# Eight transposes in two visits instead of four in four: the hand-over of finished activations in an encoder's feed-forward on one core

## The chip, the cores and the metric

One core of a Trainium2 chip. The metric is the device time of one execution in microseconds (us), as the median of runs. TensorE does the matmuls and the transposes, ScalarE (ACT in the rows) and VectorE (DVE) empty the accumulators and prepare weights, GpSimd (POOL) and SyncE (SP) issue transfers. PEld is TensorE's weight load, which runs beside its matmuls.

## What is computed

Two layers of an encoder on 512 tokens of width 1024; the first mixes the tokens by dilated window attention, the second by gated linear attention. Each mixer is followed by the same feed-forward, which the change touches:

```python
def swiglu(h, w_gate_up, w_down):
    g, u = jnp.split(h @ w_gate_up, 2, axis=-1)
    return (jax.nn.silu(g) * u) @ w_down
# every layer: h = h + mixer(rms_norm(h)); h = h + swiglu(rms_norm(h))
# FFN_HIDDEN = 2816, everything float32
```

## The kernel before

**Numbers in two halves.** A float32 operand is split into a rounded part (`wh`, `xh`; made by ScalarE, L96) and the rest (`wl`, `xl`; made by VectorE, L97), and a product is three matmuls: high by high, low by high, high by low. In `product` these are L329, L330 and L331.

**The first half of the feed-forward** is `gate_up`. The 2816 hidden columns of gate and of up are done in six chunks, j = 0 to 4 with 512 columns and j = 5 with 256. In each chunk the blocks of `h @ w_gate_up` come from seven block products instead of eight (Strassen's scheme, with sums of blocks of h, `S1` to `S4`, made beforehand, and sums of blocks of the weights, made while they load). The seven products stand in this order: A11, A12, S1, S2, S4, S3, A22. Each is 24 matmuls of 128x512 (128x256 in the last chunk) on two weight tiles of 128x1024. They share three pairs of PSUM banks: A11, S2, S3 and A22 go to `b1`, A12 to `b2` (both with the tag `pp`, printed as ppp), S1 and S4 to `b3` (tag `s`, printed as ps). Between products ScalarE copies a bank out (`copy`, L368), and VectorE combines the copies (L382, L410, L411, L420, L432). S3 and A22 are both summed into `b1`, and `b1` is copied between them: A22 may write a bank only when L368 has read it.

**The hand-over.** At the end of a chunk `done = (h1, h2)` holds its activations, tokens on the partitions. The second half of the feed-forward needs them turned. `turn(c)` does a quarter of a chunk: four transposes of 128x128 (L354, matmuls against an identity) into one PSUM bank, two of `h1` and two of `h2`, and one copy by ScalarE (L356). The bank is `pt` for even c and `po` for odd c, one buffer each. The quarters of chunk j-1 are turned during chunk j: `turn(0)` after A11, `turn(1)` after A12, `turn(2)` after S1, `turn(3)` after S2. The very last chunk's two quarters are turned at the end of `gate_up`, which the change leaves alone. Per layer that is 22 quarters, 88 transposes, on both layers 176.

**What sets the order.** Each engine works through its own instructions in a fixed order, which a scheduler sets when the program is built: among the instructions that it holds to be ready it takes the one with the highest priority, and priority falls in the order of the code. `with self.tc.issue_after(x)` makes it place the instructions inside after x. Only `turn(0)` stands in such a block (after `self.multiplied`, the last matmul of A11).

**Weights.** `forms` loads and sums the weight tiles of a chunk. Three buffers each of `wh` and `wl` go round: the split of a tile (L96, then L97) can start when the tile three places earlier has been multiplied. The tiles of S4 and S3 share their raw buffers `wB`: once S4's two tiles are split, an adding transfer issued by GpSimd (L252, for each tile when its L97 has ended) turns them into S3's, which are then split again. Chunks 1 to 4 work this way.

Of the kernel before, what the change touches and what calls it, by code (L numbers as in the profile page):

```python
# [39 lines left out]
class Trunk:  # L40
# [292 lines left out]
    def gate_up(self, layer, acts):  # L333
# [15 lines left out]
        def turn(c):  # L349
            if done is None:  # L350
                return
            pt = self.p("to"[c % 2])
            for i in range(NT):
                nc.tensor.transpose(pt[:, i * P:(i + 1) * P], done[i // 2][:, i % 2, c * P:(c + 1) * P], self.ident)  # L354
            a = self.t("h") if len(acts) < KT else late[len(acts) - KT]
            ACT(a, pt, AF.Copy)  # L356
            acts.append(a)

        for j in range(6):
# [5 lines left out]
            def copy(src):  # L365
                out = keep()
                for i in range(2):
                    self.copied = ACT(out[:, i, 0:width], src[i][:, 0:width], AF.Copy)  # L368
                return out
# [2 lines left out]
            self.product(b1, A11, first if j == 0 else next(w), width, True)  # L372
            with self.tc.issue_after(self.multiplied.ins):
                turn(0)
            g1 = copy(b1)
            b2 = pair("pp")
            self.product(b2, A12, next(w), width, True)
            turn(1)
            def gates():
                for i in range(2):  # L380
                    e = g1[:, i, 0:width]
                    DVE.tensor_add(e, b2[i][:, 0:width], e)  # L382
                    ACT(e, e, AF.Silu, scale=R[:, i:i + 1])
# [6 lines left out]
                with self.tc.issue_after(self.low.ins):  # L390
                    self.last_sums()
            self.product(b3, S1, x5, width, True)
            turn(2)
            p5 = copy(b3)
            x6 = next(w)
            if j == 0:
# [1 line left out]
                    for m in range(KT):  # L398
                        self.add_square(m, self.h[m], ("sq", "R")[m % 2])
            self.product(b1, S2, x6, width, False)  # L400
            turn(3)
            if j == 0:
                R = self.token_norm()
                with self.tc.issue_after(self.on_dve.ins):
# [821 lines left out]
```

## Time and profile before

| what | value |
|---|---|
| median of 3 runs | 1508.99 us (1508.53 to 1509.37) |
| the profiled execution, its own time | 1508.64 us |
| its span, first to last instruction | 1506.8 us |
| TensorE busy | 1491.7 us, 99% of the span |
| VectorE, ScalarE, GpSimd busy | 63%, 52%, 7% |
| granted TensorE clock, mean | 1.000 |

The span is the part of the execution in which instructions run; the 1.8 us between it and the time lie around it. A row of a timeline gives the start, the duration, the engine, the line and the operation with what it writes and reads, and in brackets the idle time of the engine before it and what ended that. Matmuls overlap: a 128x512 matmul is printed with 0.39 us and the next one starts 0.23 us later, so costs on TensorE are read from starts, not from durations.

### The profile page before, as it was taken

What the parts mean: (1) busy time and instruction counts of PE and PEld (TensorE: products, weight loads), DVE (VectorE), ACT (ScalarE), POOL (GpSimd) and SP (SyncE); (2) the same over time, 40 slices, a digit from 0 to 9 for tenths busy, and PEclk for the clock granted to TensorE, in tenths of its full rate; (3) what the DMA queues carried; (4) which work ended last, traced back from release to release, by engine and by line L of the source; (5) the groups of instructions that cost most, each with busy time, mean ns of one, the idle gap of its engine ahead of it and who ended that gap; (6) DMA issues with size and microseconds to landing.
All of it is one profiled execution on the core that took longest, in us unless ns stands there. A gap on an engine that the chain in (4) does not pass through costs nothing.

```text
span 1506.8 us, 21145 instructions
## 1 busy us (share of the span) xinstructions
PE 1491.7 (99%) x8142; PEld 1225.9 (81%) x8142; DVE 947.9 (63%) x1728; ACT 781.8 (52%) x1348; POOL 110.3 (7%) x192
## 2 busy tenths in 40 slices
PE   8999999999999999999999999999999999999998
PEld 6878787887877878888888887888888888888887
DVE  6584766777476778866667334837476866668222
ACT  6353453545466655755567233545644855568121
POOL 0001010101010010211110000000010211110000
PEclk9999999999999999999999999999999999999999
DMA  8423222243222136777674333212156676675331
GB/s 281 158 67 94 81 79 84 85 128 99 74 71 71 44 121 194 224 168 156 148 162 129 92 100 96 91 56 78 46 157 188 195 170 153 156 152 147 118 110 60
DMA packets 59829, 183.95 MB, mean 122 GB/s; under 512 B 10032, under 2 KB 10608, under 8 KB 59728
## 3 DMA queue, kind: packets, MB, share of 16 engines
q1 hardware_dynamic: 44912, 133.17, 27.0%
q0 software_dynamic: 14816, 49.42, 16.4%
q8 instruction: 64, 1.05, 0.3%
q14 instruction: 37, 0.30, 0.1%
HBM read 174.11 MB, written 8.46 MB: 121 GB/s over the span
## 4 chain that ended last, share of the span: by engine, by line
PE 87%; DVE 8%; ACT 2%; DMA 1%; issue 1%; SPq 0%; ACTq 0%; DVEq 0%
PE ppp L109 9%; PE ppp L108 9%; PE ppp L110 9%; PE ppp L549 8%; PE ppp L550 8%; PE ppp L548 8%; PE ppp L329 6%; PE ppp L330 6%; PE ppp L331 6%; PE ps L331 2%; PE ps L329 2%; PE ps L330 2%; PE po L680 2%; PE ps L640 1%; DVE wl L97 1%
## 5 line engine op out<-in xcount | busy, mean ns | idle before, releaser
L97 DVE TENSOR_TENSOR wl<-wf,wh 128x1024 fp32r<-128x1024 f32 (+1 forms) x184 | 220.6, 1200 | 229.8 <-ACT wh L96 229.0
L96 ACT ACTIVATE wh<-wf 128x1024 fp32r<-128x1024 f32 (+1 forms) x184 | 191.3, 1040 | 326.7 <-PE ppp L109 195.2
L548 PE MATMUL ppp<-wh,xs 128*128 128x512 f32 (+1 forms) x672 | 256.7, 386 | 5.5 <-ACT wh L96 5.5
L549 PE MATMUL ppp<-wl,xs 128*128 128x512 f32 (+1 forms) x672 | 257.7, 383 | 0.7 <-DVE wl L97 0.3
L550 PE MATMUL ppp<-wh,xs 128*128 128x512 f32 (+1 forms) x672 | 257.5, 383 | 0.0
L548 PEld LDWEIGHTS ppp<-wh,xs 128*128 128x128 f32 x672 | 126.6, 189 | 32.4 <-ACT wh L96 5.5
L549 PEld LDWEIGHTS ppp<-wl,xs 128*128 128x128 f32 x672 | 126.8, 189 | 26.5 <-DVE wl L97 2.9
L550 PEld LDWEIGHTS ppp<-wh,xs 128*128 128x128 f32 x672 | 126.8, 189 | 25.0 <-issue 1.3
L97 DVE TENSOR_TENSOR wl<-wA,wh 128x1024 fp32r<-128x1024 f32 x88 | 107.6, 1222 | 37.8 <-ACT wh L96 37.8
L96 ACT ACTIVATE wh<-wA 128x1024 fp32r<-128x1024 f32 x88 | 93.2, 1059 | 62.1 <-PE ppp L331 45.8
L329 PE MATMUL ppp<-wh,a 128*128 128x512 f32 (+1 forms) x288 | 108.1, 381 | 0.0
L108 PE MATMUL ppp<-xs,wh 128*128 128x512 f32 x272 | 107.4, 396 | 0.0
L330 PE MATMUL ppp<-wl,a 128*128 128x512 f32 (+1 forms) x288 | 107.4, 373 | 0.0
L331 PE MATMUL ppp<-wh,a 128*128 128x512 f32 (+1 forms) x288 | 107.3, 374 | 0.0
L109 PE MATMUL ppp<-xs,wh 128*128 128x512 f32 x272 | 106.6, 393 | 0.0
L110 PE MATMUL ppp<-xs,wl 128*128 128x512 f32 x272 | 106.0, 391 | 0.0
L97 DVE TENSOR_TENSOR wl<-wB,wh 128x1024 fp32r<-128x1024 f32 x38 | 46.5, 1225 | 73.7 <-ACT wh L96 73.7
L628 ACT ACTIVATE sm<-sm,st 128x160 f32<-128x160 f32 (+2 forms) x128 | 56.8, 447 | 40.9 <-DVE st L627 40.8
L329 PE MATMUL ps<-wh,sh 128*128 128x512 f32 (+1 forms) x192 | 73.1, 381 | 0.0
L329 PE MATMUL ppp<-wh,sh 128*128 128x512 f32 (+1 forms) x192 | 72.2, 376 | 0.0
L331 PE MATMUL ppp<-wh,sl 128*128 128x512 f32 (+1 forms) x192 | 71.6, 373 | 0.0
L331 PE MATMUL ps<-wh,sl 128*128 128x512 f32 (+1 forms) x192 | 71.5, 373 | 0.0
(319 smaller groups left out, 2955.0 us busy)
## 6 DMA issues: line engine op xcount, KB each, us to landing
wA<-in_gate_up_dram POOLq DMA_DIRECT2D x52, 512.0 KB, 5.5
wf<-in_down_dram SPq DMA_DIRECT2D x32, 512.0 KB, 3.5
wf<-in_gate_up_dram SPq DMA_DIRECT2D x24, 512.0 KB, 4.5
wf<-in_a_w_v_dram SPq DMA_DIRECT2D x20, 512.0 KB, 3.4
wB<-in_gate_up_dram POOLq DMA_DIRECT2D x20, 512.0 KB, 5.5
wf<-in_a_w_q_dram SPq DMA_DIRECT2D x16, 512.0 KB, 3.3
wf<-in_a_w_qk_dram SPq DMA_DIRECT2D x16, 512.0 KB, 3.3
wB<-in_gate_up_dram SPq DMA_DIRECT2D x16, 512.0 KB, 3.3
```

The lines of the kernel that those rows point to most:

```text
L96: nc.scalar.activation(hi, src, AF.Copy)
L97: self.low = nc.vector.tensor_sub(lo, src, hi.bitcast(F32))
L108: mm(out, lhsT=wh, rhs=xh, start=start, stop=False)
L109: mm(out, lhsT=wh, rhs=xl, start=False, stop=False)
L110: self.multiplied = mm(out, lhsT=wl, rhs=xh, start=False, stop=stop)
L329: mm(a, lhsT=xh[:, tok], rhs=wh[:, f], start=start and k == 0, stop=False, skip_group_check=True)
L330: mm(a, lhsT=xh[:, tok], rhs=wl[:, f], start=False, stop=False, skip_group_check=True)
L331: self.multiplied = mm(a, lhsT=xl[:, tok], rhs=wh[:, f], start=False, stop=k == last, skip_group_check=True)
L548: mm(a, lhsT=xh, rhs=wh[:, f], start=k == 0, stop=False)
L549: mm(a, lhsT=xh, rhs=wl[:, f], start=False, stop=False)
L550: self.multiplied = mm(a, lhsT=xl, rhs=wh[:, f], start=False, stop=k == KT - 1)
L628: nc.scalar.activation(sm[:, w], sm[:, w], AF.Exp, bias=n, scale=-1.0, accum_out=l)
```

## The change

`turn(1)` moves up from behind A12 to stand beside `turn(0)` behind A11, in the same block. `turn(3)` moves up from behind S2 to stand beside `turn(2)` behind S1, and both now stand in a block that places them after the last matmul of S1.

```diff
             with self.tc.issue_after(self.multiplied.ins):
                 turn(0)
+                turn(1)
             g1 = copy(b1)
             b2 = pair("pp")
             self.product(b2, A12, next(w), width, True)
-            turn(1)
+
             def gates():
...
             self.product(b3, S1, x5, width, True)
-            turn(2)
+            with self.tc.issue_after(self.multiplied.ins):
+                turn(2)
+                turn(3)
             p5 = copy(b3)
...
             self.product(b1, S2, x6, width, False)
-            turn(3)
```

Three places of the order of instructions show what it does. Names carry buffer numbers; `g_6609` and `g_6684` are `h1` and `h2` of chunk 1 of the first layer, `sh`, `sl` the halves of the sums S, `a_...` those of A22.

TensorE, first layer, where chunk 1 goes from S3 to A22, before:

```order
L330 MATMUL ppp_6422<-wl_6657,sh_6047 128x512
L331 MATMUL ppp_6422<-wh_6656,sl_6048 128x512
L354 MATMUL po_6812<-ident_65,g_6609 128x128
L329 MATMUL ppp_6421<-wh_6689,a_5872 128x512
L330 MATMUL ppp_6421<-wl_6690,a_5872 128x512
```

and with the change:

```order
L330 MATMUL ppp_6422<-wl_6657,sh_6047 128x512
L331 MATMUL ppp_6422<-wh_6656,sl_6048 128x512
L329 MATMUL ppp_6421<-wh_6689,a_5872 128x512
L330 MATMUL ppp_6421<-wl_6690,a_5872 128x512
L331 MATMUL ppp_6421<-wh_6689,a_5873 128x512
```

Before, the scheduler has pulled the first transpose of the next chunk's `turn(1)` forward, from behind A12 to between S3 and A22. It does so at this place in chunks 1 to 4 of both layers, eight times, and once more, in the second layer, in the middle of a product of chunk 1. With the change these nine single transposes are gone from there and stand with the others behind A11.

TensorE, the end of S1 in chunk 2 of the first layer, before:

```order
L331 MATMUL ps_6824<-wh_6835,sl_6048 128x512
L354 MATMUL pt_6863<-ident_65,g_6609 128x128 x2
L354 MATMUL pt_6863<-ident_65,g_6684 128x128 x2
L329 MATMUL ppp_6726<-wh_6875,sh_5894 128x512
L330 MATMUL ppp_6726<-wl_6876,sh_5894 128x512
```

and with the change:

```order
L331 MATMUL ps_6824<-wh_6835,sl_6048 128x512
L354 MATMUL pt_6863<-ident_65,g_6609 128x128 x2
L354 MATMUL pt_6863<-ident_65,g_6684 128x128 x2
L354 MATMUL po_6870<-ident_65,g_6609 128x128 x2
L354 MATMUL po_6870<-ident_65,g_6684 128x128 x2
L329 MATMUL ppp_6726<-wh_6882,sh_5894 128x512
```

The four transposes into `po` stood 24 matmuls further down, behind S2. Over chunks 1 to 5 of both layers the order has 45 separate stops for transposes between matmuls before, besides the nine single ones, and 23 with the change: two in a chunk, but three in chunk 1 of the first layer (six, two and eight transposes) and four in chunk 1 of the second.

ScalarE, chunk 3 of the first layer, from the end of S1 to the end of S2, before:

```order
L368 ACTIVATE g_7172<-ps_7126 128x512
L96 ACTIVATE wh_7220<-wB_7130 128x1024
L356 ACTIVATE xs_6083<-pt_7166 128x512
L368 ACTIVATE g_7172<-ps_7127 128x512
L96 ACTIVATE wh_7224<-wB_7132 128x1024
L368 ACTIVATE g_7215<-ppp_7031 128x512
L96 ACTIVATE wh_7258<-wB_7130 128x1024
L356 ACTIVATE xs_6084<-po_7209 128x512
```

and with the change:

```order
L368 ACTIVATE g_7178<-ps_7126 128x512
L96 ACTIVATE wh_7220<-wB_7130 128x1024
L356 ACTIVATE xs_6083<-pt_7166 128x512
L356 ACTIVATE xs_6084<-po_7172 128x512
L368 ACTIVATE g_7178<-ps_7127 128x512
L96 ACTIVATE wh_7224<-wB_7132 128x1024
L368 ACTIVATE g_7215<-ppp_7031 128x512
L96 ACTIVATE wh_7258<-wB_7130 128x1024
```

The copy of `po` moves up three places, ahead of the second copy of `b3` and of the second split of S4's weights. VectorE's order changes only in that one split (L97) moves ahead of a combining step (L411) it stood behind, and in that, in the last chunk, a split for the second half (L448) moves by one or two places; the transfers of SP and GpSimd keep their order, and no instruction is added or removed on any engine.

## Rows read from the trace of the kernel before

**Rows 1.** Page, part 1: busy us (share of the span) x instructions, by engine.

```profile
PE 1491.7 (99%) x8142; PEld 1225.9 (81%) x8142; DVE 947.9 (63%) x1728; ACT 781.8 (52%) x1348; POOL 110.3 (7%) x192
```

**Rows 2.** Timeline of PE, four transposes behind A12 in chunk 1, first layer.

```profile
639.05 0.39 PE L331 MATMUL ppp<-wh,a 128*128 128x512 f32 x1
639.28 0.60 PE L354 MATMUL po<-ident,g 128*128 128x128 f32 x4
639.64 0.48 PE L329 MATMUL ps<-wh,sh 128*128 128x512 f32 x1
639.95 0.40 PE L330 MATMUL ps<-wl,sh 128*128 128x512 f32 x1
```

**Rows 3.** Timeline of PE, one transpose between matmuls, chunk 1, second layer.

```profile
1204.53 0.27 PE L354 MATMUL pt<-ident,g 128*128 128x128 f32 x1
...
1204.88 0.40 PE L329 MATMUL ppp<-wh,a 128*128 128x512 f32 x1
```

**Rows 4.** Timeline of PE, six transposes to two banks, end of the first layer's gate_up.

```profile
812.81 0.49 PE L354 MATMUL pt<-ident,g 128*128 128x128 f32 x3
813.14 0.49 PE L354 MATMUL po<-ident,g 128*128 128x128 f32 x3
...
813.70 0.39 PE L109 MATMUL ppp<-wA,wh 128*128 128x512 f32 x1
```

**Rows 5.** Timeline of PE, PEld and the wait, one single transpose between S3 and A22.

```profile
662.47 0.27 PE L354 MATMUL po<-ident,g 128*128 128x128 f32 x1
...
662.98 0.40 PE L330 MATMUL ppp<-wl,a 128*128 128x512 f32 x1
...
662.64 0.19 PEld L329 LDWEIGHTS ppp<-wh,a 128*128 128x128 f32 x1 [0.25 <-ACT g L368]
```

**Rows 6.** Timeline of PE, a wait for L368 in A22 with no transpose in it.

```profile
1194.62 0.39 PE L330 MATMUL ppp<-wl,a 128*128 128x512 f32 x1
1194.99 0.50 PE L329 MATMUL ppp<-wh,a 128*128 128x512 f32 x1
1195.33 0.39 PE L330 MATMUL ppp<-wl,a 128*128 128x512 f32 x1
```

**Rows 7.** PE, PEld: last of the eight singles before A22; waits of PEld, 1194:1383.

```profile
1352.88 0.27 PE L354 MATMUL po<-ident,g 128*128 128x128 f32 x1
...
PEld ppp L330 <- DVE wl L97: 0.3, 1, 0.3
```

**Rows 8.** Timeline of PE and PEld, last transpose of turn(0), chunk 1, first layer.

```profile
633.75 0.40 PE L330 MATMUL ppp<-wl,a 128*128 128x512 f32 x1
...
634.49 0.39 PE L329 MATMUL ppp<-wh,a 128*128 128x512 f32 x1
...
634.09 0.14 PEld L354 LDWEIGHTS pt<-ident,g 128*128 128x128 f32 x1 [0.38 <-DVE g L432]
```

**Rows 9.** Timeline of PE, turn(0) behind A11 in chunk 5, first layer.

```profile
791.74 0.49 PE L354 MATMUL pt<-ident,g 128*128 128x128 f32 x3
...
792.83 0.33 PE L354 MATMUL pt<-ident,g 128*128 128x128 f32 x1 [0.36 <-DVE g L432]
```

**Rows 10.** Timelines of ACT, POOL, DVE, PEld: S4's second tile and S3's, chunks 2 and 3.

```profile
688.85 1.06 ACT L96 ACTIVATE wh<-wB 128x1024 fp32r<-128x1024 f32 x1 [1.15 <-issue]
...
691.46 0.86 POOL L252 DMA_DIRECT2D wB<-in_gate_up_dram  x1 [2.32 <-DVE wl L97]
...
738.58 1.23 DVE L97 TENSOR_TENSOR wl<-wB,wh 128x1024 fp32r<-128x1024 f32 x1 [1.48 <-ACT wh L96]
...
740.15 0.19 PEld L330 LDWEIGHTS ppp<-wl,sh 128*128 128x128 f32 x1
```

**Rows 11.** Timeline of PE with granted clock: a run of eight, then four transposes, in attention.

```profile
475.47 1.09 PE L640 MATMUL ps<-ident,sm 128*128 128x128 f32 x8
476.40 0.60 PE L698 MATMUL pt<-ident,ob 128*128 128x128 f32 x4
476.93 1.09 PE L680 MATMUL po<-pt,v 128*64 128x128 f32 x16
...
475.00:477.00 2.00, 2.00 (x17) 1.45 (x17) 0.60 (x1) 2.00 (x5) 0.30 (x2) 1.00 0.21 80
```

## The prediction

> **What bounds the kernel now.** First the busy times: TensorE is busy for 99% of the span [rows 1], so only what lengthens or shortens its own row of starts counts, and of the other engines only what makes it wait. Then its timeline at the places of the change. The reader is to see there what a stop for transposes costs. In steady work one 128x512 matmul starts 0.23 us after the other. Behind A12 [rows 2] the first of four transposes takes the place of the next matmul, at 639.28. The next matmul is printed at 639.64, but the true cost shows one later: the second matmul starts at 639.95, 0.67 us after the first transpose, where it would have started after 0.23. Four transposes cost 0.44 us. By the same reading a single one costs 0.35 - 0.23 = 0.12 [rows 3], and six to both banks, `pt` and `po` in one row, 0.89 - 0.23 = 0.66 [rows 4]. A straight line through these has 0.108 us for each transpose and 0.012 for each stop. That is the core of the matter: **a stop has almost no price of its own**, so stopping less often has almost nothing to give.
>
> Third, the timelines of TensorE and its weight load around the nine single transposes. Between S3 and A22 the first matmul of A22 must wait until ScalarE has copied the bank (L368). The single transpose stands in that wait [rows 5]: from its start to the second matmul behind it 0.51 us, 0.28 more than the 0.23 of undisturbed work, and the weight load is still idle for 0.25 until L368 ends. A wait for L368 that holds no transpose [rows 6] costs 1195.33 - 1194.62 - 2 x 0.23 = 0.25. So the transpose in the wait costs 0.03 at most and is as good as free. This holds eight times, the last at 1352.88, and the ninth stands before a wait for a split (L97) of 0.3 us [rows 7].
>
> **The change, part by part.**
>
> *Nine hidden transposes come into the open.* They leave the waits, which stay as long as they were, since L368 and L97 do not depend on them, and join a stop behind A11. There each costs 0.108 us. For two of them, those of chunk 5, there is new cover. In chunk 5 the last transpose of `turn(0)` waits for L432, the step that finishes `h2`: with only a 128x256 product ahead it is reached too early [rows 9], at 792.83 after 0.36 us of standstill. Before, three transposes and two matmuls fill the time from 791.74; now it is six transposes (0.65), then the same wait, then two. Counted over both stops, seven transposes before and eight now end at the same time within 0.02 us. So seven pay: 7 x 0.108 = +0.76 us.
>
> *Fewer stops.* 45 become 23: 22 x 0.012 = -0.26 us.
>
> *One wait filled.* In chunk 1 of the first layer the last transpose of `turn(0)` waits for L432: the two starts around it [rows 8] lie 0.74 apart, 0.46 for two matmuls and 0.12 for the transpose, so 0.16 is wait. With the change six transposes and a matmul stand ahead of it instead of three and two, 0.1 us more, and L432 comes in time or nearly. -0.16 at most, nothing at least; I take -0.12, since 0.1 of 0.16 and some of the rest is covered.
>
> *ScalarE's copies.* `po` is copied 5 us sooner and straight behind `pt`. That pushes the second copies of `b1` and `b3` and the splits behind them back by one L356, some 0.5 us. A bank is next written one or two products later, 5.5 us (24 x 0.23) or more, so no matmul waits for that: 0. `turn(0)` and `turn(2)` use the same bank, two products and 11 us apart, so the one buffer of `pt` and of `po` is free in time: 0.
>
> *Weights.* Here the change adds delay. A split waits for the tile three places earlier; the second tile of S4 for the first tile of S2. With eight transposes ahead of S2 instead of four, S2 runs 0.44 us later, against S4 and S3, which keep their places. S4's second split (688.85 [rows 10]) moves with it, so does the adding transfer that GpSimd issues when that split has ended (691.46), and so does the last link, the split of S3's second tile. In chunk 3 that last split ends at 738.58 + 1.23 = 739.81, and TensorE loads it at 740.15: 0.34 us of slack against 0.44 of delay. In chunk 3 a wait of 0.1 appears, with the refill that such a wait brings (in [rows 6] 0.25 in all). That is the least slack of the eight chunks that work this way; in the others the same two instructions lie further apart. I take +0.25 for one wait; the ends are 0 (the transfer lands as much sooner as it is issued late) and 8 x 0.35 = +2.8 (all eight are just late).
>
> *The longer run.* A run of eight transposes does not occur in this stage. Elsewhere eight take 476.40 - 475.47 = 0.93 us [rows 11], 0.116 each, against 0.108 from the line. The change makes 18 runs of eight (two of them with the wait for L432 inside), which would cost 18 x 8 x 0.008 = +1.2 at that end; below, the line itself is the end, as nothing shows a transpose under it. I take the line, since [rows 4] with both banks is the nearest, and keep +1.2 for the range.
>
> The Trainium skill (TensorE: Matmul & The Clock Gate, section "Back-to-back issue gap") gives some 81 ns for a pair of weight load and matmul at 128 columns, in a sustained stream. The rows here show 108 to 116 ns for float32 transposes, and the measurement decides; by that figure of the Trainium skill the seven in the open would be an estimated +0.57, and the sum +0.25 instead of +0.63 us.
>
> **Sum:** 0.76 - 0.26 - 0.12 + 0.25 = +0.63 us. On the profiled execution's 1508.64 us that is 1509.3. The median of the runs lies 0.35 above that execution, at 1508.99, so the forecast is **1509.6 us**: less than 0.2% (3.0 us, about what a measurement of this kernel can tell from no change) above before.
>
> **The rivals.**
>
> *Slower: the chain of S3's weights gives way.* The mechanism is the one above: S2's first tile is released 0.44 us later, and split, transfer and split again must fit into what is left. It decides where the slack falls under 0.44 us; one chunk shows 0.34. Against it: in most chunks more is left, and a late split only moves TensorE by the part that is missing. For it: a transfer's landing varies by some tenths, and ScalarE and VectorE also have other work in between. If the chain were late by 0.5 us in all eight chunks, with 0.15 for the refill, that is 8 x 0.65 = 5.2 us: 1514.2.
>
> *Faster: a stop has a price that the single transposes do not show.* Behind four transposes the second matmul comes 0.31 after the first instead of 0.23 [rows 2], as if each return to matmuls cost 0.08. Then 22 stops fewer give -1.8 instead of -0.26: 1508.1. Against it: the single stop [rows 3], with the same return, costs 0.12 in all.
>
> *The nine were not hidden.* If L368 came sooner without the transpose in front of it, nothing is lost by moving them out: 0.63 - 0.76 = -0.13, 1508.9. Against it: L368 waits for the last matmuls of S3, which stand ahead of the transpose.
>
> *The clock.* Eight transposes could lower TensorE's clock from its upper level, 2.4 GHz, to 1.2: 18 runs of 0.87 us would take twice as long, +15.7 us on the sum's 0.63: 1525.3. Against it: in attention twelve transposes in a row run at a granted clock of 1.00, behind matmuls [rows 11]. The Trainium skill (TensorE: Matmul & The Clock Gate, section "Part 4: PE-mode transpose") says that transposes do not count as work for the clock. By that rule this rival would be the likelier; the trace speaks against it for runs of this length.
>
> **How the numbers follow.** Forecast 0.70; slower by S3's weights 0.08; faster by the price of a stop 0.12; not hidden 0.09; clock 0.01. The predicted time is the likeliest, 1509.6. Its own range is 1508.7 (no late weights, the price of a stop twice what I take, a median 0.3 lower) to 1511.2 (plus 1.2 for the longer run and a few late splits). The whole range takes in the next two cases below, 1508.0, and a little of the chain above, 1511.8. Faster by over 0.2% (under 1506.0) needs more than any case gives: 0.03. Slower (over 1512.0) takes the chain, the clock and a part of the upper bounds: 0.09. Within 0.2%: 0.88.
>
> **What would show it.** Right: 160 transposes in chunks 1 to 5, sixteen clean runs of eight at 0.87 to 0.93 us each; between S3 and A22 no transpose, and the wait for L368 as long or longer in the weight load's rows, 0.35 instead of 0.25; TensorE's busy time and span within 1 us of before; chunk 2 to chunk 3 some 0.1 us further apart. The chain shows as waits of L330 or L329 for L97 or L96 in S3's second tile. Wrong: waits at those places in many chunks; a run of eight far from 0.9 us; a granted clock under 1.00 anywhere; or a span that is more than 2 us shorter, for which I have no mechanism.

## The result, and the profile after

The changed kernel takes 1511.93 us (median of 14 runs, 1510.04 to 1513.74) against 1509.11 for the kernel before (14 runs on the same chips): ratio 1.0019, 95% interval 1.0012 to 1.0027. It is slower by some 2.8 us. The forecast was 1509.6 with a range up to 1511.8: the time lies just above the range, and the slow-down is more than four times the forecast's +0.63.

The profiled execution of the changed kernel took 1513.74, its span is 1511.9, against 1508.64 and 1506.8. It is one of the two longest of the 14, so it shows what can go wrong rather than the usual amount. Lines below have moved by one or two: L382, L410, L411, L420 and L432 of before are L383, L412, L413, L422 and L434 now.

First the page, part 1, which answers to [rows 1].

```profile
PE 1494.9 (99%) x8142; PEld 1227.0 (81%) x8142; DVE 948.0 (63%) x1728; ACT 781.8 (52%) x1348; POOL 110.3 (7%) x192
```

TensorE's busy time grew by 3.2 us with the same 8142 instructions (matmuls overlap, so rows that stand further apart count as more busy time), and the span by 5.1; the weight load's grew by 1.1, the other engines' by 0.1 at most. So TensorE did not get more work, its rows were pulled apart. Where?

**Not in the visits.** Timeline of TensorE, the eight transposes behind A11 in chunk 2 of the first layer (it answers to [rows 2]):

```profile
674.48 0.39 PE L331 MATMUL ppp<-wh,a 128*128 128x512 f32 x1
674.72 0.60 PE L354 MATMUL pt<-ident,g 128*128 128x128 f32 x4
675.15 0.60 PE L354 MATMUL po<-ident,g 128*128 128x128 f32 x4
675.51 0.48 PE L329 MATMUL ppp<-wh,a 128*128 128x512 f32 x1
675.82 0.40 PE L330 MATMUL ppp<-wl,a 128*128 128x512 f32 x1
```

From the first transpose to the second matmul behind them 1.10 us, less 0.23: eight cost 0.87, 0.109 each. Four cost 0.44, so two visits of four and one of eight differ by 0.01.

**Not at the boundary that lost its transpose.** TensorE and its weight load, S3 to A22 in chunk 1 (it answers to [rows 5]):

```profile
663.24 0.39 PE L331 MATMUL ppp<-wh,sl 128*128 128x512 f32 x1
663.64 0.50 PE L329 MATMUL ppp<-wh,a 128*128 128x512 f32 x1
663.98 0.40 PE L330 MATMUL ppp<-wl,a 128*128 128x512 f32 x1
...
663.64 0.19 PEld L329 LDWEIGHTS ppp<-wh,a 128*128 128x128 f32 x1 [0.43 <-ACT g L368]
```

From the last matmul of S3 to the second of A22 0.74 us, of which 0.46 is work: the wait for L368 costs 0.28, as it did with the transpose in it. The weight load now stands for 0.43 where it stood for 0.25. The transposes were hidden there, as forecast.

**In waits for weights.** The waits of the weight load by what it waited for, first layer's gate_up and second layer's (us in all, times, longest). Of waits for a split (L96, L97) the kernel before has in the same views only the one of [rows 7], in chunk 1 of the second layer.

```profile
PEld ppp L329 <- ACT g L368: 1.9, 5, 0.4
PEld ppp L330 <- DVE wl L97: 1.7, 5, 0.5
PEld pt L354 <- DVE g L434: 1.1, 2, 0.9
...
PEld ppp L330 <- DVE wl L97: 2.7, 5, 1.1
PEld ppp L329 <- ACT g L368: 2.3, 6, 0.4
PEld pt L354 <- DVE g L434: 0.9, 1, 0.9
PEld ppp L329 <- ACT wh L96: 0.7, 1, 0.7
```

The longest stand in S3 of chunk 4, second layer. Rows of GpSimd, ScalarE, VectorE, the weight load and TensorE there:

```profile
1345.21 0.86 POOL L252 DMA_DIRECT2D wB<-in_gate_up_dram  x1 [2.75 <-DVE wl L97]
...
1352.56 1.06 ACT L96 ACTIVATE wh<-wB 128x1024 fp32r<-128x1024 f32 x1 [3.84 <-DMA wB<-in_gate_up_dram]
...
1353.65 1.23 DVE L97 TENSOR_TENSOR wl<-wB,wh 128x1024 fp32r<-128x1024 f32 x1 [4.16 <-ACT wh L96]
...
1353.67 0.19 PEld L329 LDWEIGHTS ppp<-wh,sh 128*128 128x128 f32 x1 [0.70 <-ACT wh L96]
1354.93 0.19 PEld L330 LDWEIGHTS ppp<-wl,sh 128*128 128x128 f32 x1 [1.07 <-DVE wl L97]
...
1353.00 0.39 PE L331 MATMUL ppp<-wh,sl 128*128 128x512 f32 x1
1353.67 0.50 PE L329 MATMUL ppp<-wh,sh 128*128 128x512 f32 x1 [0.28 <-ACT wh L96]
1354.93 0.50 PE L330 MATMUL ppp<-wl,sh 128*128 128x512 f32 x1 [0.76 <-DVE wl L97]
1355.27 0.39 PE L331 MATMUL ppp<-wh,sl 128*128 128x512 f32 x1
```

The adding transfer for S3's second tile is issued at 1345.21 and has landed when ScalarE can split the tile, at 1352.56: 7.35 us later. The split's two halves follow, TensorE waits for both, and 1353.00 to 1355.27, 2.27 us, holds three matmuls' worth of work: 1.6 us lost. This is the chain of S3's weights, the rival on the slow side. The same tile in the kernel before, rows of GpSimd, ScalarE, VectorE and the weight load:

```profile
1341.66 0.86 POOL L252 DMA_DIRECT2D wB<-in_gate_up_dram  x1 [2.32 <-DVE wl L97]
...
1347.42 1.06 ACT L96 ACTIVATE wh<-wB 128x1024 fp32r<-128x1024 f32 x1 [1.34 <-DMA wB<-in_gate_up_dram]
...
1348.51 1.23 DVE L97 TENSOR_TENSOR wl<-wB,wh 128x1024 fp32r<-128x1024 f32 x1 [2.14 <-ACT wh L96]
...
1350.16 0.19 PEld L330 LDWEIGHTS ppp<-wl,sh 128*128 128x128 f32 x1
```

There the transfer takes 5.76 us, 1.59 less. Against A22 the change issues it 0.47 later (10.91 us ahead instead of 11.38 in chunks without waits), so most of what TensorE loses here is the late landing, and less than a third of it is the late issue.

To compare executions I use two distances. A chunk's length runs from the first matmul of A22 in the chunk before it to its own: 40.2 us before, in chunks 2 to 4 of both layers. The stage is the first layer from its first transpose in chunk 1 to the first matmul of the second half behind the last chunk's first transposes (633.19 to 813.38 in the trace of before) and the second layer from A22 of chunk 0 to the same point (1191.67 to 1383.48): 180.19 + 191.81 = 372.00 before, 375.67 with the change. Of these 3.67, chunk 4 of the second layer has 1.74 (41.96 against 40.22), chunk 3 of the first 0.56 (40.75 against 40.19; waits of 0.42 and 0.34 in S3), the two chunks 5 together 0.90 (25.76 and 26.13 against 25.34 and 25.65; some 0.36 of it is A22 of the second layer's chunk 4, which waits for a split and counts in the next chunk's length). The rest, 0.47, is transposes in the open and waits in A22. Another 1.15 us lie ahead of the first changed instruction (634.34 against 633.19), and 0.33 between the two layers' stages.

### The profile page after: what moved, and what is told of

Read it like the earlier page. It is cut to its first block, busy times and chain, and to the rows that moved or that the text cites. A ratio compares the mean times of both kernels' runs of the same rounds, so it can differ in the third digit from the quotient of the medians.

```text
span 1511.9 us, 21140 instructions
## 1 busy us (share of the span) xinstructions
PE 1494.9 (99%) x8142; PEld 1227.0 (81%) x8142; DVE 948.0 (63%) x1728; ACT 781.8 (52%) x1348; POOL 110.3 (7%) x192
## 3 DMA queue, kind: packets, MB, share of 16 engines
q8 instruction: 64, 1.05, 0.3%
## 4 chain that ended last, share of the span: by engine, by line
PE 86%; DVE 8%; ACT 2%; issue 2%; DMA 1%; SPq 0%; ACTq 0%; DVEq 0%
PE ppp L109 9%; PE ppp L108 9%; PE ppp L110 9%; PE ppp L551 8%; PE ppp L552 8%; PE ppp L550 8%; PE ppp L329 6%; PE ppp L330 6%; PE ppp L331 6%; PE ps L331 2%; PE ps L329 2%; PE ps L330 2%; PE po L682 2%; PE ps L642 1%; DVE wl L97 1%
## 5 line engine op out<-in xcount | busy, mean ns | idle before, releaser
L97 DVE TENSOR_TENSOR wl<-wf,wh 128x1024 fp32r<-128x1024 f32 (+1 forms) x184 | 220.4, 1199 | 229.0 <-ACT wh L96 228.3
L96 ACT ACTIVATE wh<-wf 128x1024 fp32r<-128x1024 f32 (+1 forms) x184 | 191.3, 1040 | 325.8 <-PE ppp L109 199.6
L97 DVE TENSOR_TENSOR wl<-wA,wh 128x1024 fp32r<-128x1024 f32 x88 | 107.4, 1220 | 37.6 <-ACT wh L96 37.6
L96 ACT ACTIVATE wh<-wA 128x1024 fp32r<-128x1024 f32 x88 | 93.1, 1059 | 60.9 <-PE ppp L331 43.1
L97 DVE TENSOR_TENSOR wl<-wB,wh 128x1024 fp32r<-128x1024 f32 x38 | 46.5, 1225 | 79.7 <-ACT wh L96 79.7
L330 PE MATMUL ppp<-wl,sh 128*128 128x512 f32 (+1 forms) x192 | 71.7, 373 | 0.8 <-DVE wl L97 0.8
```

The costliest lines, as they stand in the source:

```text
L96: nc.scalar.activation(hi, src, AF.Copy)
L97: self.low = nc.vector.tensor_sub(lo, src, hi.bitcast(F32))
L330: mm(a, lhsT=xh[:, tok], rhs=wl[:, f], start=False, stop=False, skip_group_check=True)
```

## The experiments

The change has two halves: the first pair (it takes the single transposes out of the waits and changes what A22 multiplies when) and the second pair (it makes S2 start 0.44 us later). Diffs are against the kernel before unless said otherwise. "S3 waits" counts the chunks, of the eight in an execution (1 to 4 of both layers), in which the weight load is idle for 0.15 us or more for a split in S3, "A22 waits" those in which it is for L97 in A22. The weight load runs ahead of the matmuls, so that some 0.1 of such an idle time costs TensorE nothing.

| kernel (runs of it) | S2 | singles hidden | ratio to before, 95% | stage, us | S3 waits | A22 waits |
|---|---|---|---|---|---|---|
| before (3 traces) | 0 | yes | | 372.00, 371.77, 371.66 | 0 of 24 | 0 of 24 |
| the change (3) | late | no | 1.0019 (1.0012 to 1.0027), 1.0029 (1.0018 to 1.0040) | 375.67, 378.56, 374.75 | 6 of 24 | 21 of 24 |
| first pair alone (2) | 0 | no | 1.0010 (1.0001 to 1.0018), 1.0007 (0.9998 to 1.0016) | 372.81, 372.35 | 3 of 16 | 3 of 16 |
| second pair alone (4) | late | yes | 1.0015 (1.0006 to 1.0024), 1.0011 (1.0002 to 1.0020) | 372.56, 372.79, 372.57, 374.18 | 1 of 32 | 0 of 32 |
| four visits, none hidden | 0 | no | 1.0014 (1.0005 to 1.0022) | 375.24 | 2 of 8 | 3 of 8 |
| the change, A22's order edged (2) | late | no | 1.0019 (1.0009 to 1.0028), 1.0021 (1.0011 to 1.0031) | 373.00, 374.32 | 2 of 16 | 0 of 16 |
| first pair, A22's order edged | 0 | no | 1.0006 (0.9997 to 1.0015) | 373.34 | 1 of 8 | 0 of 8 |
| the change, second pair behind S2 | early | no | 1.0005 (0.9996 to 1.0013) | 371.94 | 2 of 8 | 4 of 8 |
| S2 early | early | yes | 1.0001 (0.9992 to 1.0009) | 372.38 | 1 of 8 | 0 of 8 |
| singles hidden, S2 early | early | yes | 0.9999 (0.9990 to 1.0008) | 372.13 | 2 of 8 | 0 of 8 |

An interval is some 1.3 us to either side, so neighbours in this table do not part by their times; the times part the change from the last three rows, and the traces say why. In the first row of A22's order edged, 373.00 has only four transposes instead of six ahead of its end in each layer, so some 0.4 has to be added to it to compare.

The three traces of the change, by the starts of the matmuls: S3's waits cost TensorE 2.1, 4.5 and 1.3 us, A22's 1.1, 1.7 and 1.0, of stages that are 3.9, 6.8 and 2.9 longer than the mean of before. That leaves some 0.6 for chunk 5 and the transposes in the open.

### The halves apart

First pair alone:

```diff
             with self.tc.issue_after(self.multiplied.ins):
                 turn(0)
+                turn(1)
...
-            turn(1)
```

> Only the first pair is joined: turn(0) and turn(1) stand behind A11, turn(2) and turn(3) stay behind S1 and S2. S2 starts when it did before, so S3's weights are not delayed, but the single transposes are gone and A22's order is the one of the changed kernel (low half of the second weight tile as 8th matmul). Measure: the five chunk periods of both layers (first transposing stop of chunk 1 to that of the tail), 359.4 us before, 363.0 with the change (+3.65). Theory 1 (S2 late, then the adding transfer, S3's second split and what stands behind it on VectorE): +0.6 to +0.8, the exposed transposes alone; no wait of TensorE for a split in S3, none above 0.1 in A22. Theory 2 (A22's order alone makes TensorE wait): +1.5 to +2.5, with waits for L97 at A22's 8th matmul of 0.2 to 0.5. Theory 3 (the run of eight itself is dearer): half of the changed kernel's +3.65, about +1.8, and no waits. The time: 1509.5 to 1510 by theory 1, 1510.5 to 1511.5 by 2 and 3.

Measured: 1510.88, ratio 1.0010. The stage is 0.8 longer than the first trace of before. S3's *first* tile waits 0.33 in chunk 1 and 0.20 in chunk 3 of the first layer, and A22 of the same two chunks 0.31 and 0.29. Chunks without such waits take 40.26 to 40.29, as the seven transposes in the open ask for. Theory 1 has the size of the stage, but not the waits: it had none in S3. (All waits in this part are idle times of the weight load.)

Second pair alone:

```diff
-            turn(2)
+            with self.tc.issue_after(self.multiplied.ins):
+                turn(2)
+                turn(3)
...
-            turn(3)
```

> Only the second pair is joined: turn(2) and turn(3) behind S1; turn(1) stays behind A12, so the single transposes stay hidden between S3 and A22 and A22 keeps the order of before (low half of the second tile as 14th matmul). S2 is late by four transposes, 0.44 us, as in the changed kernel. Theory 1: the adding transfer is issued 0.4 to 0.5 later against A22 (10.9 instead of 11.4 us ahead of it), waits for L96 or L97 of 0.3 to 1 us at S3 in one to three of the eight chunks, and A22's second L97 0.4 late, but with 1.4 us of room, so no waits in A22: chunk periods +0.5 to +2.0. Theory 2: no wait in A22, and the periods as before, -0.2 to +0.3 (no transposes come into the open). Theory 3: +1.8, in the stops. The time: 1509.6 to 1511 by theory 1, 1509 by theory 2, 1511 by theory 3.

> The second pair alone once more. Its profiled execution was its fastest of 11 (1510.1, up to 1514.0) and showed no wait in S3; the median is 0.8 above. If S2's delay works through S3's second tile, a median execution shows it: the second adding transfer 10.9 us ahead of A22 and, in one or two chunks, waits for L96 or L97 at S3's second tile of 0.3 to 1.5 us in all, which the three executions of before never show. If there is none here either, the second pair's cost lies elsewhere: in chunk 5, where the last transpose of turn(0) waits 0.9 to 1.0 for L433 instead of 0.6 to 0.9 for L432.

> The second pair alone a third time, for the trace of an execution in the upper half of its times (over 1511.0; 11 of 22 lie there, and both profiled ones lay at the low end, 1510.1 and 1508.8, with no wait in S3). By theory 1 an execution over 1511 has waits for L96 or L97 in S3, at the second tile, that make up most of what it is longer than 1509; one under 1510.5 has none.

> The second pair alone a fourth time, for the same end: over 1511 us with waits for L96 or L97 at S3's second tile of most of the surplus, or under 1510.5 without; over 1511 without them speaks against theory 1.

Measured: 1510.91 and 1511.27 in the two timed comparisons; traces of executions of 1510.10, 1508.84, 1510.08 and 1510.79. The adding transfer for S3's second tile is issued 10.9 to 11.2 us ahead of A22 where nothing holds up TensorE, 11.4 before, in all four: the delay is there in every chunk. In the first three executions the waits in S3 that theory 1 expected do not come; what the delay does there is small, and it shows in two places. One is the single transpose, which is no longer free. TensorE, chunk 3 of the first layer, the second execution:

```profile
742.03 0.39 PE L331 MATMUL ppp<-wh,sl 128*128 128x512 f32 x1
742.62 0.30 PE L354 MATMUL po<-ident,g 128*128 128x128 f32 x1 [0.20 <-DVE g L412]
742.68 0.48 PE L329 MATMUL ppp<-wh,a 128*128 128x512 f32 x1
743.00 0.39 PE L330 MATMUL ppp<-wl,a 128*128 128x512 f32 x1
```

The transpose waits for L412, the step of VectorE that finishes `h1`, and the boundary costs 0.51 instead of 0.28. The other is chunk 5, where the last transpose of `turn(0)` waits 0.91 to 1.05 for VectorE instead of 0.47 to 0.86 and the chunk takes 25.7 to 25.8 instead of 25.3 to 25.7. The fourth execution has the wait I was looking for, in chunk 1. GpSimd, ScalarE and the weight load:

```profile
648.08 0.85 POOL L252 DMA_DIRECT2D wB<-in_gate_up_dram  x1 [1.42 <-DVE wl L97]
651.71 0.85 POOL L252 DMA_DIRECT2D wB<-in_gate_up_dram  x1 [2.77 <-DVE wl L97]
...
655.06 1.06 ACT L96 ACTIVATE wh<-wB 128x1024 fp32r<-128x1024 f32 x1 [3.38 <-DMA wB<-in_gate_up_dram]
658.64 1.06 ACT L96 ACTIVATE wh<-wB 128x1024 fp32r<-128x1024 f32 x1 [2.03 <-DMA wB<-in_gate_up_dram]
...
657.44 0.19 PEld L330 LDWEIGHTS ppp<-wl,sh 128*128 128x128 f32 x1 [0.47 <-DVE wl L97]
661.02 0.19 PEld L330 LDWEIGHTS ppp<-wl,sh 128*128 128x128 f32 x1 [0.97 <-DVE wl L97]
```

Both transfers land 7.0 and 6.9 us after their issue, where the three other executions have 5.8 and 5.4, and the stage is 1.5 longer. So this half can have the wait in S3, but as an event of some executions, in one chunk of 32, and the delay of S2 is not what makes it frequent: kernels with S2 late have it in 9 chunks of 72, the other changed ones, with S2 in its place or early, in 11 of 56. No execution over 1511 was caught in a trace, and what fills the slower half of its runs was not seen.

### The kernels again

> The changed kernel once more, for a second profiled execution and for a time on the chip of the runs sent with it. If the waits come from a chain whose last link is a transfer that lands now sooner, now later, the same chain of instructions shows with other lengths: the adding transfer 10.9 us ahead of A22 again, but waits in S3 in other chunks than 3 (first layer) and 4 (second layer), from none to 2 us in all. If they come from the order alone, the same waits of the same lengths in the same chunks. The time 1511.5 to 1512.5 either way, chunk periods +1.5 to +4 against before.

> The kernel before once more, for a second profiled execution. In six of the eight runs so far TensorE waits in chunk 3 of the first layer for S3's weights, 0.2 to 2 us, also where S2 is not late (four visits unhidden: 1.7 us; S2 early: 0.85 us), because the first adding transfer lands 6.5 to 8.4 us after its issue there instead of the 6.3 of the profile of before. If those waits come from the change or from the edits, this execution shows none: landing 6.2 to 6.5 in chunk 3, chunk periods 359.4 us within 0.3. If they come with the transfers in every kernel and the profile of before was a lucky one, there is a wait of 0.2 to 1 us here too, and the first feed-forward visit starts 0.3 to 1.2 later than 633.2.

> The same again, as the run before this one: by the one reading no wait for L97 or L96 in S3, chunk periods 359.4 within 0.3; by the other a wait of 0.2 to 1 us in chunk 3 of the first layer in at least one of the two.

> The changed kernel a third time. In the two executions so far S3 waits in chunk 3 of the first layer (0.76 and 2.2 us) and in chunk 4 of the second (1.77 and 1.66 us), at the second tile each time among others, and A22 waits in five or six of eight chunks. If chunk 4 of the second layer is a regular outcome of S2's delay there: 1.5 us or more again. If both were chance: chunk periods within 1 us of before's plus 1.

Measured: the change 1513.13 (7 runs, up to 1517.31), ratio 1.0029; its traced executions 1517.31 and 1512.48. The kernel before 1508.95 and 1508.92, the first visit at 633.7 and 633.8. The stage of before repeats within 0.34 us, with no wait in S3; the waits of the change move about: chunks 1, 3 (first layer) and 4 (second) in the second trace, chunk 1 alone in the third, where chunk 4 of the second layer takes 40.40. So the waits come with the edits, and not in the same chunks each time. That the first trace of before was a lucky one is not borne out by the two more. But the traced executions of the change lie above the medians of its runs, and those of before under theirs, so 6 of 24 against 0 of 24 makes the difference look larger than it is in the middle of the runs.

### What the first half costs, and through what

Four visits, each in a block behind its product, none pulled forward:

```diff
-            turn(1)
+            with self.tc.issue_after(self.multiplied.ins):
+                turn(1)
...
```

and the same for `turn(2)` and `turn(3)`.

> The kernel before with turn(1), turn(2) and turn(3) each in a block behind the product where they stand: four visits of four, none joined, but no single transpose between S3 and A22 any more, and A22 in the order of the changed kernel. S2 stays where it was. If joining the first pair is free and only what it uncovers costs, this is the first pair's run over again: +1.5 us, 1510.9 (its time), with short waits at A22's 8th matmul. If the run of eight itself costs, or TensorE's standing still in front of a longer visit, this is nearer before: +0.76 by the transposes alone, 1510.1. If neither, 1509.4.

Measured: 1511.54, ratio 1.0014, waits in S3 of chunk 3 of the first layer (0.80 and 0.91) and chunk 2 of the second (0.26), and A22's 8th matmul waiting 0.29 to 0.53 in three chunks. It is no faster than the first pair joined, though none of its visits is joined. What the first half costs does not come from joining.

A22's order, put back by an edge (two lines of it), on the change and, in chunks 1 to 4 only, again on the change and on the first pair:

```diff
+                with self.tc.issue_after(second.ins) if hold and k > 1 else ExitStack():
...
-            self.product(b1, A22, x4, width, False)
+            self.product(b1, A22, x4, width, False, hold=True)
```

`second` is the first matmul on the second bank; with `hold` the third k step and all behind it follow that. Two matmuls of the next chunk's A11 are then placed in the gap.

> The changed kernel, with one thing put back: an edge in A22's product holds its third k step and what follows behind the first matmul on the second bank, so the low half of the second weight tile is multiplied later in A22, about as before. The eight transposes and S2's delay stay as in the changed kernel. Theory 1 with theory 2 as its second step (VectorE's splits are 0.4 us late, and A22 asks for the second one 1.4 us earlier): waits for L97 in A22 of 0.16 to 0.55 go, the waits in S3 stay; chunk periods +2.2 to +2.8 instead of +3.65 against before. Theory 1 alone: +3 to +3.7, for the wait moves to the next matmul that needs the late split. Theory 3: +3.65, unchanged.

> As the run on A22's order, with the edge only in chunks 1 to 4, so that chunk 0 of the second layer does not wait 0.96 us for a split as it did there (that cost 0.54 of its own). No wait for L97 in A22, S3's as the transfers land. If A22's order matters beside S2's delay: under the changed kernel in the same call by 0.3 to 1 us. If the split is late in any case and the wait only moves: equal within 0.3.

> The first pair joined, the second as before, so S2 is where it was; and the edge in A22's product in chunks 1 to 4, so that the low half of the second weight tile is not the 8th matmul. Against the first pair alone in the same call: if A22's order is what the first pair costs beyond its seven transposes in the open, 0.3 to 0.9 us faster, 1510.0 to 1510.5, no wait for L97 in A22. If the cost is the splits of S3 that come late because the two adding transfers of A22's tiles follow each other sooner (2.62 us apart in chunk 1 of the first layer instead of 3.56) and the next one lands later (6.9 us after its issue instead of 5.9): equal within 0.3, with waits in S3 in chunk 1 and 3 of the first layer.

> The first pair alone once more, beside the run before it on the same chip. 1510.5 to 1511.3. In chunk 1 of the first layer the adding transfers of A22's tiles 2.62 us apart and S3's first landing 6.5 to 7.4 us after its issue, a wait there at S3's first tile again; gate_up 0.5 to 2 us longer than in the three executions of before (342.2 to 342.6 from the first A22 of each layer to the second half). If the first pair's waits were chance: as before plus the transposes, +0.6, and no wait in S3.

Measured: 1511.86 and 1512.26 on the change (the change beside the second 1513.13), 1510.27 on the first pair (1510.37 without the edge, beside it). The waits in A22 are gone in all three, and in the second of these chunks 2 to 4 of both layers, but for one of 41.92, take 40.19 to 40.22, as before; in the trace that is up to 0.4 us less for a chunk than in the change. But S3's waits stay, in one chunk of each, and the times do not part from those without the edge. The first pair again, without the edge, has a wait of 0.21 in chunk 3 of the first layer and none in chunk 1, where the expectation had one: the landing there is 5.94 us after the issue, not 6.5 to 7.4. A22's order is a part of the loss, not its cause. The first run's edge also made chunk 0 of the second layer wait 0.96 for a split.

Why does S3's first tile wait, whose chain the change does not delay? Chunk 1 of the first layer, GpSimd's adding transfers and ScalarE's split of S3's first tile, before (second trace):

```profile
642.74 0.85 POOL L252 DMA_DIRECT2D wA<-in_gate_up_dram  x1 [13.08 <-DVE wl L97]
646.30 0.85 POOL L252 DMA_DIRECT2D wA<-in_gate_up_dram  x1 [2.72 <-DVE wl L97]
648.57 0.85 POOL L252 DMA_DIRECT2D wB<-in_gate_up_dram  x1 [1.42 <-DVE wl L97]
...
654.47 1.06 ACT L96 ACTIVATE wh<-wB 128x1024 fp32r<-128x1024 f32 x1 [2.74 <-DMA wB<-in_gate_up_dram]
```

and with the change (third trace):

```profile
643.42 0.85 POOL L252 DMA_DIRECT2D wA<-in_gate_up_dram  x1 [13.44 <-DVE wl L97]
646.04 0.85 POOL L252 DMA_DIRECT2D wA<-in_gate_up_dram  x1 [1.77 <-DVE wl L97]
648.76 0.85 POOL L252 DMA_DIRECT2D wB<-in_gate_up_dram  x1 [1.87 <-DVE wl L97]
...
656.14 1.06 ACT L96 ACTIVATE wh<-wB 128x1024 fp32r<-128x1024 f32 x1 [3.78 <-DMA wB<-in_gate_up_dram]
```

Without the four transposes between A12 and S1, two tiles are released nearer to each other, and the two transfers of A22's tiles follow at 2.62 us instead of 3.56. The third then lands 7.38 us after its issue instead of 5.90. Of ten executions with the spacing of 2.62 in this chunk nine have 6.5 to 7.4; of nine with 3.56 eight have 5.8 to 6.0, and one (above) 7.0. But the spacing alone does not do it. In chunks 2 and 4 of the first layer and 1 and 3 of the second, transfers that follow each other at the same 2.6 and 2.7 us have S3's first tile ready after 5.3 to 5.6 in 36 cases of 38; and in chunk 3 the landing varies from 6.3 to 8.4 among kernels that have almost the same spacing.

What the slow chunks share is another transfer. Among the DMA packets of every trace is one of 16 KB, of the queue that the page calls `instruction`, at the same four places: it starts between 7.2 us ahead of S4's first matmul and 1.9 behind it in chunks 1 and 3 of the first layer and 2 and 4 of the second, and in none of the other four (two of which have one of 8 KB). The queues in the third trace of the change (packets, MB, share of 16 engines), chunk 1 of the first layer (641.9 to 660.0) and chunk 4 (764.6 to 782.7):

```profile
q0 software_dynamic: 576, 2.10, 65.8%
q1 hardware_dynamic: 27, 0.11, 3.0%
q8 instruction: 1, 0.02, 0.8%
...
q0 software_dynamic: 745, 2.72, 84.6%
```

All 20 chunks with a wait in S3, over all traces, are among the 76 with such a packet. Of the 152 transfers of S3's tiles in these, 75 are ready more than 6.0 us after the issue and 37 more than 6.5; of the 152 in the other 76 chunks 2 and none. The kernel before has the packet too, and its slower landings, up to 6.5, are in the same four chunks. So the place of the waits goes with this packet. How it holds up the transfers, and why with the change the landings reach 7.7 where before's end at 6.5, no run here tests.

### Both costs taken out

The second pair behind S2 instead of S1, the rest as in the change:

> The changed kernel with the second pair behind S2 instead of S1: as many stops, as many runs of eight, as many transposes in the open, but S2 starts 0.44 us earlier than before instead of 0.44 later, and S4 and S3 stay where they were. Theory 1: the adding transfer is issued 0.4 earlier than before against A22 (11.8 us ahead of it), no wait for a split in S3, VectorE's splits of A22 early enough for its 8th matmul: chunk periods +0.3 to +0.8, 1509.3 to 1509.9. Theory 2: the waits at A22's 8th matmul stay, +1.5 to +2.5. Theory 3: as the changed kernel, +3.65, 1511.9.

S2 early alone, `turn(2)` moved beside `turn(3)` behind S2:

```diff
-            turn(2)
...
+            turn(2)
             turn(3)
```

> The kernel before with turn(2) moved from behind S1 to behind S2, beside turn(3): first pair, single transposes and A22's order as before, and S2 0.44 us earlier. With the run of the second pair behind S1 (S2 0.44 late, +1.5 us) this is the other side of the same dose. Theory 1: the adding transfer 11.8 us ahead of A22; fewer and shorter waits for late landings than before: 1508.9 to 1509.4, and a highest run under before's. If the cost of the second pair was its run of eight and not S2's delay: +1.5 here too, 1510.9.

And the two visits of eight with both costs removed:

```diff
-            with self.tc.issue_after(self.multiplied.ins):
-                turn(0)
+            turn(0)
+            turn(1)
...
-            turn(1)
...
-            turn(2)
...
-            turn(3)
+            with self.tc.issue_after(self.multiplied.ins):
+                turn(2)
+                turn(3)
```

> Both costs taken out of the change, two visits of eight kept: turn(0) and turn(1) behind A11 but without the block, so that one single transpose is again pulled forward between S3 and A22 and A22 keeps the order of before; turn(2) and turn(3) behind S2, so that S2 is 0.44 us earlier than before. If the two effects are all that the change costs: as before or 0.2 better, 1509.2 to 1509.7. If joining the visits costs by itself: +1 or more, 1510.5.

Measured: 1510.13 (ratio 1.0005), 1509.46 (1.0001) and 1509.00 (0.9999). With S2 early and the singles hidden, two visits of eight take the time of the kernel before. The traces of these have waits in S3 too, 0.40 and 0.16 in the first (chunk 3 of the first layer, chunk 2 of the second; its expectation by theory 1 had none there or in A22), 0.85 in chunk 3 of the second and 0.18, 0.50 and 0.75 in chunks 1 and 3 of the last. With S2 early the transfers of S3's two tiles are issued 2.72 us apart instead of 3.19. In chunk 3 of the first layer they are then ready 6.7 to 7.4 us after the issue (before: 5.7 to 6.5), and it is the first tile, issued as before, that waits; in chunk 4, without the packet, the same spacing has 5.3 to 5.5. Chunk 5 of the first layer is 0.4 to 0.5 shorter (24.8 to 24.9), that of the second 0.2 to 0.5 longer. No version beats the kernel before by more than can be measured.

## Why the prediction was wrong

- **Price of a transpose, of a stop, of a long run:** right. Eight cost 0.87 (forecast 0.87 by the line), 0.01 is what a stop costs, and the end of the range for longer runs, +1.2, was not needed. The estimate of +0.57 from the Trainium skill (TensorE: Matmul & The Clock Gate, section "Back-to-back issue gap") for the seven in the open rests on 81 ns; the rows have 109, and the measurement decides. By its own terms the sum with +0.57 would have been +0.44, not the +0.25 that the prediction gives.
- **Nine hidden transposes come into the open:** right in kind. The boundary costs 0.28 with and without, and clean chunks grow by 0.0 to 0.1.
- **New cover in chunk 5:** wrong. The text had both versions "end at the same time within 0.02 us", on the assumption that L432 ends when it did. In the change it ends 0.4 later against A22 (the second L434 starts at 794.38, 9.15 behind A22's first matmul; L432 at 792.02, 8.75 behind it), and the last transpose of `turn(0)` waits 0.90 in the weight load's rows instead of 0.56. The two chunks 5 together take 51.6 to 52.0 us in the three traces of the change, 50.6 to 51.0 in the three of before; in the second layer a part of that is A22's wait in chunk 4.
- **Wait on L432 in chunk 1 filled:** right. 0.17 of waiting is left of 0.38, and the stretch from there to A22 is 0.15 shorter where S3 does not wait (29.30 against 29.45), forecast 0.12.
- **ScalarE's copies:** nothing seen against 0.
- **Clock:** right. Granted 1.00 in the mean, the upper level, and 0.999 or more in every run of the change; the rule of the Trainium skill that transposes do not count as work for the clock (same page, "Part 4: PE-mode transpose") changed nothing at eight in a row.
- **Weights: this is the step that failed.** "S2 runs 0.44 us later", and with it the adding transfer: measured, 10.9 instead of 11.4 us ahead of A22. But the sum took "+0.25 for one wait", from one chunk's slack of 0.34, as if only S3's second tile could be late and only by the part of S2's delay that the slack did not cover. S3's waits cost 1.3 to 4.5 us in the three traces, and three things were wrong with the term.
  1. The slack was read in one execution as if the landing were fixed. Landings behind the two transfers of S3 range from 5.2 to 8.4 us over all traces. In the three traces of the change S3 waits in six chunks of 24, and such a chunk is 0.5 to 2.1 us longer, not 0.35. Of the 7.9 us that these waits cost in the three traces 2.8 stand at S3's first tile, whose chain S2's delay does not touch; at the second tile the delay of 0.47, an estimate from the same starts, can account for 2.5 at most. The larger part is landings later than any of before. Chunk 4 of the second layer, late in the first two traces, had a slack of 0.42 in the trace of before (its last split ends at 1349.74, TensorE loads it at 1350.16), less than the delay of 0.44, and the prediction counted only the chunk with the least.
  2. Everything behind that split on VectorE's queue is late as well, in all eight chunks: L412, L413, A22's second split, L422, L434. That is what chunk 5 pays and the single transposes of the second pair pay.
  3. With the singles gone the scheduler also takes the low half of A22's second weight tile as the 8th matmul, where it had been the 14th, 1.4 us sooner. The prediction did not count it. With S2 in its place or early it waits less often: in 3 chunks of 16 with the first pair, 3 of 8 with four visits, 4 of 8 with the second pair behind S2. With S2 late and the old order it never waits (none in 32). With both it is 21 in 24, at 1.0 to 1.7 us in a trace. VectorE's row in chunk 3 (the split that A22 waits for) and the wait:

```profile
745.35 1.22 DVE L97 TENSOR_TENSOR wl<-wA,wh 128x1024 fp32r<-128x1024 f32 x1
...
746.62 0.19 PEld L330 LDWEIGHTS ppp<-wl,a 128*128 128x128 f32 x1 [0.55 <-DVE wl L97]
```

The rival "S3's weights chain gives way" had the mechanism and a chance of 0.08. It came in part: not all eight chunks late by 0.5 us each, but some chunks late by up to 2. The prediction's bound of +2.8 for this step has the size of the slow-down by chance: it was eight waits of 0.35, and what came is one to three of 0.5 to 2.1, with A22 and chunk 5 beside them. The range (to 1511.8) left most of it out. That was the error of judgement: a chain that misses by 0.1 in a trace with varying landings should not have been given 0.08.

What stays open: why the time ahead of the first changed instruction varies from 632.7 to 635.2 us between executions (all three of the change lie at 634.0 or later, all three of before at 633.8 or earlier, but the orders are the same up to there and other kernels lie on both sides), and what makes the landings in the four chunks with the `instruction` packet so much later in the changed kernels than before.

## What to carry to other kernels

Moving work on the busiest engine changes nothing in its sum and still moves the times at which all others are released: follow each tile that the moved work stands in front of, through split, transfer and split again, down the whole queue of the engine that does the last step, and not only to the first reader. A slack against a transfer is a distribution: take the landing times of every repetition in the trace, here 5.3 to 6.3 us in the one trace, where one value was used (and even that was too narrow: with the change they reach 7.7), and price a miss at what a late landing costs, not at the missing tenth. Two small shifts that are each covered can share one cover; check the sum of delays where the change touches both the producer's time and the consumer's place in the order.

## What had not been expected of the hardware

The adding transfers of S3's tiles, 512 KB each and issued by GpSimd, lie 0.86 us in its row, and the data is ready 5.2 to 8.4 us after the issue. How close they follow each other does not settle it: at 2.6 and 2.7 us they are ready after 5.3 to 5.6 in most of the chunks in which no 16 KB packet of the `instruction` queue falls among them. Where one does, 75 of 152 take more than 6.0 us, elsewhere 2 of 152. The Trainium skill (DMA: Bandwidth & Descriptors, section "Anatomy of one DMA — SWDGE (gpsimd) path") has a fixed part and one that grows with the bytes, an estimate of 3.2 us for 512 KB by its fit; the rows here are longer and differ among transfers of one size, and the measurement decides.
